# A hybrid conv and dilated-attention encoder: transpositions of the identity ahead of the stretches of products, and an attention core of three borders per head

## The chip, the cores and the metric

The kernel runs on one core of one Trainium2 chip. The metric is the device time of one execution in microseconds (us). The engines are TensorE (PE, with PEld for its weight loads), VectorE (DVE), ScalarE (ACT), GpSimd (POOL) and SyncE (SP), which issues the loads of the weights.

## What is computed

The input is x, 256 tokens of 2048 values, all in float32. Two layers follow, each with a mixer and a gated MLP; then a last norm.

```python
def reference(x, ...):
    for i in range(DEPTH):                      # 2
        h = rmsnorm(x, mix_norm_g[i])
        if i % N_MIXERS == 0:
            x = x + short_conv_mixer(h, ...)    # 2048 -> 6144, conv of width 3, gates, -> 2048
        else:
            x = x + dilated_attention_mixer(h, ...)
        h = rmsnorm(x, ffn_norm_g[i])
        x = x + conv_ffn(h, ...)                # 2048 -> 11264, conv, silu(a) * b, 5632 -> 2048
    return rmsnorm(x, final_norm_g)
```

The attention has 16 heads of 128 values and 3 groups with dilations 1, 4 and 16. Each group has its own q, k and v; scores have an ALiBi bias and a window, and the groups' outputs are mixed by their softmax denominators. The kernel does this as one softmax over 512 columns per query block.

## The kernel before, in words

**Products.** A float32 product is made of three fp32r products: each operand is split into a rounded part and its remainder. `split` (lines 76 to 80) makes the parts: ACT casts (L77), DVE subtracts (L78). `load_w` (82 to 91) loads 1 MB of weights with SP and splits it in two halves of 8 blocks of 128x128, each in one of four `w2` buffers. `mm` (98 to 112) runs over these: per half 8 products high by high (L107), 8 high by low (L109), 8 low by high (L111), each 128x128 by 128x256. So a unit of weights with 16 blocks is 48 products. In the short convolution and in the MLPs the moving operand is `h`, `y` or `a`, always 256 columns of a tile with 512.

**The stages, in order.** `short_conv` (175 to 241): a first block of three outputs while data arrive (`mm1`, L94 to L96), then 45 units over `h` and 16 over `y`. `ffn` (283 to 328) for layer 0: 4 chunks of 22 units over `h` (`up`) and 16 units of 33 products over `a` (`down`), one chunk behind. `attention` (331 to 504). `ffn` for layer 1.

**The norms.** `rms` (161 to 169) sums the squares with one plain float32 matmul (ones by `acc`, 128x256, L163; two records in the profile) and takes the root on DVE and ACT. It stands in the short convolution after its second unit, in each MLP and at the attention's start after the first unit; the products don't wait for it, since its factor is applied to their results.

**Attention.** For each pair of heads there are three `v_unit`s (351 to 385; 96 products each, with weights as the moving operand and `h` as the stationary one, L369 and L374), then twelve `qk_unit`s (387 to 399; 48 products each). The work of a head on scores is queued as tasks, one of which is taken after each unit by `step`: `scores` for group 0 (three fp32r products for each of two query blocks, L404 to L406), `scores` for groups 1 and 2 (two plain float32 matmuls each, 128x128, L418, four records), `softmax` (420 to 431; DVE and ACT only, L423 to L430), `transposes` for each query block (433 to 446; four transpositions of 128x128 float32 to PSUM, L437, copied out by ACT and DVE), and `pv` (448 to 464; six fp32r products, L455, four plain float32 matmuls, L460, eight records, and two copies). A head so interrupts the stream of units six times. `step(3)` after each of the first two units of the output projection and a last loop end the tasks of head 15; then the projection's 16 units over `o`.

**What sets the order.** The kernel is a program of tiles: each engine's order comes from a planner that walks the instructions by their place in the program and takes what it holds to be ready; waits follow from the tiles. `tc.issue_after(ins)` puts an instruction behind another on its engine. The PSUM tile `pt` has one buffer, `s` two, `ps` four, `ot` one.

Of the kernel before, what the change touches and what calls it, by code (L numbers as in the profile page):

```python
# [16 lines left out]
P = 128  # L17
# [21 lines left out]
def encoder_kernel(ctx: ExitStack, tc: tile.TileContext, xT, gs, scw, fcw, dist, w_first, w_in, w_so, w_v, w_qk, w_ao, w_up, w_dn, out):  # L39
# [73 lines left out]

    tp.tile([P, TPAD], F32, name="padt", tag="padt", bufs=1)

    def new_ps():
        return pp.tile([P, 2 * T], F32, name="ps", tag="ps", bufs=4)[:, :T]

# [41 lines left out]

    def rms():
        ps = pp.tile([P, 2 * T], F32, name="stat", tag="s", bufs=2)
        pe.matmul(ps[:, :T], ones, acc, start=True, stop=True)  # L163
        v = tp.tile([P, T], F32, name="v", tag="tmp", bufs=1)
        dve.tensor_scalar(v, ps[:, :T], 1.0 / D, EPS, op0=ALU.mult, op1=ALU.add)
        sd = tp.tile([P, T], F32, name="sd", tag="sq")
        act.activation(sd, v, AF.Sqrt)
        dve.reciprocal(rr, sd)
        newton(rr, v, tp.tile([P, T], F32, name="t", tag="sq"))

    def add_to_x(ps, j):
        dve.tensor_add(x[:, j, :], x[:, j, :], ps)
# [2 lines left out]
    def short_conv():  # L175
        with tc.tile_pool(name="sc", bufs=1) as sp:
            y = sp.tile([P, KT, 2 * T], F32R, name="y")

            def gate(j, es):
                u, c, b = es  # L180
# [24 lines left out]
            for j in range(1, KT):  # L205
                es = []
                for part in range(3):
                    w = load_w(w_in[3 * j + part - 3], KT)
                    if j == 1 and part == 0:
                        first = []  # L210
                        for i in range(3):
                            e = tp.tile([P, T], F32, name="e", tag=f"e{i}")
                            act.copy(e, pss[i])
                            first.append(e)
                        with tc.issue_after(ins.ins):
                            for k in range(KT):
                                squares(k)
                    ps = new_ps()
                    ins = mm(ps, w, h, range(KT))
                    if j == 1 and part == 1:  # L220
                        with tc.issue_after(ins.ins):
                            rms()
                        for e in first:
                            dve.tensor_mul(e, e, rr)
                        gate(0, first)
                        nc.sync.dma_start(fcw_sb, fcw)
                    if j == 1 and part == 0:
                        e = tp.tile([P, T], F32, name="e", tag="e0")
                        act.copy(e, ps)
                        es.append(e)  # L230
                        continue
                    if j == 1 and part == 1:
                        dve.tensor_mul(es[0], es[0], rr)
                    es.append(scaled(ps, f"e{part}", rr))
                gate(j, es)
# [47 lines left out]
    def ffn(l, nxt, halves):  # L283
        with tc.tile_pool(name=f"ff{l}", bufs=1) as sp:

            def up(c):
                a = sp.tile([P, CH, 2 * T], F32R, name="a", tag="a", bufs=2)
                for i in range(CH):
                    f = c * CH + i
                    cs = []  # L290
                    for part in range(2):
                        w = load_w(w_up[l, 2 * f + part], KT)
                        ps = new_ps()
                        mm(ps, w, h, range(KT))
                        if f == 0 and part == 0:
                            rms()
                        e = scaled(ps, f"e{part}", rr)
                        cv = sp.tile([P, T], F32, name="cv", tag=f"cv{part}", bufs=2)
                        conv(cv, e, fcw_sb[:, l, part * NF + f, :])
                        if part == 0:  # L300
                            act.activation(cv, cv, AF.Silu)
                        cs.append(cv)
                    dve.tensor_mul(cs[0], cs[0], cs[1])
                    split(a[:, i, :T], a[:, i, T:], cs[0])
                return a

            def down(c, a):
                for j in range(KT):
                    w = load_w(w_dn[l, c, j], CH)
                    ps = new_ps()  # L310
                    if c == NCH - 1 and nxt == 4:
                        last(ps, w, a, j)
                        continue
                    mm(ps, w, a, range(CH))
                    add_to_x(ps, j)
                    if c == NCH - 1:
                        ready(j, nxt, halves)

            a = up(0)
            for c in range(1, NCH):  # L320
                b = up(c)
                down(c - 1, a)
                a = b
            if nxt == 4:

                warm = tp.tile([P, 2], F32, name="warm", tag="den")
                act.activation(warm, f32(a[:, CH - 1, :2]), AF.Sqrt, bias=eps[:, 0:1], scale=0.0)
            down(NCH - 1, a)


    def attention():
        with tc.tile_pool(name="att", bufs=1) as sp:
            o = sp.tile([P, H, 2 * T], F32R, name="o")
            ds = sp.tile([P, 2, 2 * T], F32, name="ds")
# [13 lines left out]
                    pe.transpose(ps[:, :P], rp[:, i * P : (i + 1) * P], ident)  # L348
                    dve.tensor_copy(rc[:, i : i + 1], ps[:, 0:1])

            def v_unit(hp, g):

                first = hp == 0 and g == 0
                if g == 0:
                    v = sp.tile([P, 2, 2, T], F32R, name="v", tag="v0", bufs=2)
                else:
                    v = sp.tile([P, 2, T], F32, name="v", tag=f"v{g}", bufs=2)
                ps = [new_ps(), new_ps()]
                for k0 in range(0, KT, 8):
                    raw = wp.tile([P, 8, T], F32, name="rawv", tag="raw", bufs=RAW)  # L360
                    nc.sync.dma_start(raw, w_v[3 * hp + g, :, k0 * T : (k0 + 8) * T])
                    for k1 in range(k0, k0 + 8, 4):
# [8 lines left out]
                                    )  # L371
                        for k in range(k1, k1 + 4):
                            for i in range(2):
                                pe.matmul(  # L374
                                    ps[i], h[:, k, T + i * P : T + (i + 1) * P], w2[:, k - k1, 0, :],
                                    start=False, stop=k == KT - 1,
                                )
                if first:
                    norms()
                for i in range(2):  # L380
                    e = tp.tile([P, T], F32, name="e", tag="e0") if g == 0 else v[:, i, :]
                    act.mul(e, ps[i], rc[:, i : i + 1])
                    if g == 0:
                        split(v[:, i, 0, :], v[:, i, 1, :], e)
                vs[hp, g] = v

            def qk_unit(hd, g, part):
                w = load_w(w_qk[(hd * G + g) * 2 + part], KT)
                ps = new_ps()
                mm(ps, w, h, range(KT))  # L390
                r = rp if part else rq
                if g == 0:
                    e = scaled(ps, "e1", r)
# [2 lines left out]
                else:  # L396
                    t = sp.tile([P, T], F32, name="qkf", tag=f"qkf{part}", bufs=3)
                    scaled(ps, "e1", r, t)
                heads[hd, g, part] = t

            def mm3(out, l, lc, r, rc_, start, stop):
                lh, ll = l[:, lc], l[:, lc.start + T : lc.stop + T]
                rh, rl = r[:, rc_], r[:, rc_.start + T : rc_.stop + T]
                pe.matmul(out, lh, rh, start=start, stop=False)  # L404
                pe.matmul(out, lh, rl, start=False, stop=False)  # L405
                pe.matmul(out, ll, rh, start=False, stop=stop)  # L406

            def scores(hd, g):
                q, k = heads.pop((hd, g, 0)), heads.pop((hd, g, 1))
# [2 lines left out]
                for i in range(2):  # L412
                    s = heads[hd][i]
                    c = slice(i * P, (i + 1) * P)
                    if g == 0:
                        mm3(s[:, :T], q, c, k, slice(0, T), True, True)
                    else:
                        pe.matmul(s[:, T + (g - 1) * P : T + g * P], q[:, c], k[:, c], start=True, stop=True)  # L418

            def softmax(hd, i):  # L420
                s = heads[hd][i]
# [26 lines left out]
            def pv(hd):  # L448
# [7 lines left out]
                for g in (1, 2):  # L456
                    v = vs[hd // 2, g]
                    for i in range(2):
                        q = slice(i * P, (i + 1) * P)
                        pe.matmul(ot[:, q], v[:, i, c], tf[:, g - 1, q], start=False, stop=g == 2 and i == 1)  # L460
                hi, lo = (o[:, hd, z : z + T].rearrange("p (m i) -> p i m", i=2) for z in (0, T))
                src = ot.rearrange("p (i m) -> p i m", i=2)
                act.copy(hi, src)
                dve.tensor_sub(lo, src, f32(hi))

            def step(n=1):
                for _ in range(n):
                    if tasks:
                        tasks.popleft()()

            for hp in range(H // 2):
                for g in range(G):
                    v_unit(hp, g)
                    step()
                for hd in (2 * hp, 2 * hp + 1):
                    for g in range(G):
                        qk_unit(hd, g, 0)
                        step()
                        qk_unit(hd, g, 1)
                        step()  # L480
                        tasks.append(lambda hd=hd, g=g: scores(hd, g))
                    tasks.append(lambda hd=hd: (softmax(hd, 0), softmax(hd, 1)))
                    tasks.append(lambda hd=hd: transposes(hd, 0))
                    tasks.append(lambda hd=hd: transposes(hd, 1))
                    tasks.append(lambda hd=hd: pv(hd))
            first = []
            for j in range(2):
                w = load_w(w_ao[j], KT)
                ps = new_ps()
                mm(ps, w, o, range(KT - 1))  # L490
                step(3)
                first.append((ps, w))
            while tasks:
                step()
            for j in range(KT):
                if j < 2:
                    ps, w = first[j]
                    mm(ps, w, o, range(KT - 1, KT))
                else:
# [4 lines left out]
                ready(j, 3, False)  # L504

    short_conv()
    ffn(0, 2, True)
    attention()
    ffn(1, 4, False)


# [80 lines left out]
```

## Time and profile before

| | |
|---|---|
| median of 3 runs | 2787.13 us (2785.28 to 2811.06) |
| profiled execution, device time | 2787.24 us |
| its span, first to last instruction | 2784.0 us |
| mean granted TensorE clock | 0.998 |
| PE, DVE, ACT busy share of the span | 99%, 65%, 49% |
| HBM | 186 GB/s over the span |

A row of the timeline gives start, length, engine, line, operation and operands, and the count of instructions merged in it; the length runs to the end of the last one, and matmuls overlap, so the pace is read from starts. In a row of the chain the length is the time from one step to the next, so the lengths add up. In a row of the windows, the number behind x counts every instruction that lies in the stretch, those cut by its edges too.

### The profile page before, as it was taken

What the parts mean: (1) busy time and instruction counts of PE and PEld (TensorE: products, weight loads), DVE (VectorE), ACT (ScalarE), POOL (GpSimd) and SP (SyncE); (2) the same over time, 40 slices, a digit from 0 to 9 for tenths busy, and PEclk for the clock granted to TensorE, in tenths of its full rate; (3) what the DMA queues carried; (4) which work ended last, traced back from release to release, by engine and by line L of the source; (5) the groups of instructions that cost most, each with busy time, mean ns of one, the idle gap of its engine ahead of it and who ended that gap; (6) DMA issues with size and microseconds to landing.
All of it is one profiled execution on the core that took longest, in us unless ns stands there. A gap on an engine that the chain in (4) does not pass through costs nothing.

```text
span 2784.0 us, 55141 instructions
## 1 busy us (share of the span) xinstructions
PE 2766.3 (99%) x24020; PEld 2763.4 (99%) x24020; DVE 1802.8 (65%) x2553; ACT 1354.9 (49%) x1860; POOL 0.7 (0%) x6
## 2 busy tenths in 40 slices
PE   9999999999999999999999999999999999999998
PEld 8999999999999999999999999999999999999998
DVE  7666677775767757555555555555677775766755
ACT  6444455554545546444444444444455554544545
POOL 0000000000000000000000000000000000000000
PEclk9999999999999999999999999999999999999999
DMA  7555555556556556555554555555455556556554
GB/s 263 183 190 188 182 194 190 195 173 220 193 171 214 173 192 219 184 178 168 179 184 167 179 172 180 169 180 176 172 183 197 196 171 212 196 171 221 178 182 143
DMA packets 79874, 520.41 MB, mean 187 GB/s; under 512 B 9104, under 2 KB 10256, under 8 KB 28816
## 3 DMA queue, kind: packets, MB, share of 16 engines
q1 hardware_dynamic: 79488, 516.37, 54.0%
q8 instruction: 187, 3.06, 0.4%
q10 hardware_dynamic: 144, 0.52, 0.0%
q14 instruction: 55, 0.45, 0.0%
HBM read 514.76 MB, written 2.10 MB: 186 GB/s over the span
## 4 chain that ended last, share of the span: by engine, by line
PE 98%; DVE 1%; DMA 0%; issue 0%; ACT 0%; SPq 0%; DVEq 0%; ACTq 0%
PE ps L107 29%; PE ps L111 29%; PE ps L109 29%; PE ps L369 6%; PE ps L374 3%; PE ot L460 1%; PE s L418 1%; PE pt L437 1%; PE ot L455 0%; DMA raw<-in_w_first 0%; DVE x L278 0%; DVE acc L147 0%; PE s L405 0%; PE s L406 0%; PE s L404 0%
## 5 line engine op out<-in xcount | busy, mean ns | idle before, releaser
L78 DVE TENSOR_TENSOR w<-raw,w 128x1024 fp32r<-128x1024 f32 (+1 forms) x954 | 1082.3, 1135 | 689.2 <-ACT w L77 677.7
L77 ACT CAST w<-raw 128x1024 fp32r<-128x1024 f32 (+1 forms) x954 | 930.1, 980 | 1116.0 <-PE ps L111 895.7
L107 PE MATMUL ps<-h,w 128*128 128x256 f32 x5072 | 692.7, 279 | 0.0
L111 PE MATMUL ps<-h,w 128*128 128x256 f32 x5072 | 686.3, 278 | 0.0
L109 PE MATMUL ps<-h,w 128*128 128x256 f32 x5072 | 686.1, 278 | 0.0
L107 PEld LDWEIGHTS ps<-h,w 128*128 128x128 f32 x5072 | 630.1, 188 | 0.2
L109 PEld LDWEIGHTS ps<-h,w 128*128 128x128 f32 x5072 | 629.5, 188 | 0.0
L111 PEld LDWEIGHTS ps<-h,w 128*128 128x128 f32 x5072 | 629.3, 188 | 0.0
L111 PE MATMUL ps<-a,w 128*128 128x256 f32 x1408 | 201.3, 276 | 0.0
L107 PE MATMUL ps<-a,w 128*128 128x256 f32 x1408 | 201.2, 276 | 0.0
L109 PE MATMUL ps<-a,w 128*128 128x256 f32 x1408 | 201.2, 276 | 0.0
L369 PE MATMUL ps<-w2v,h 128*128 128x256 f32 x1536 | 194.1, 279 | 0.0
L78 DVE TENSOR_TENSOR w2v<-rawv,w2v 128x1024 fp32r<-128x1024 f32 x96 | 117.5, 1224 | 115.8 <-ACT w2v L77 115.8
L369 PEld LDWEIGHTS ps<-w2v,h 128*128 128x128 f32 x1536 | 184.0, 188 | 0.1
L111 PEld LDWEIGHTS ps<-a,w 128*128 128x128 f32 x1408 | 178.6, 188 | 0.0
L107 PEld LDWEIGHTS ps<-a,w 128*128 128x128 f32 x1408 | 178.6, 188 | 0.0
L109 PEld LDWEIGHTS ps<-a,w 128*128 128x128 f32 x1408 | 178.6, 188 | 0.0
L77 ACT CAST w2v<-rawv 128x1024 fp32r<-128x1024 f32 x96 | 100.7, 1049 | 123.2 <-PE ps L374 78.8
L122 DVE TENSOR_TENSOR e<-ps,rr 128x256 f32<-128x256 f32 x220 | 93.4, 425 | 57.0 <-PE ps L111 51.1
L127 ACT ACTIVATE cv<-e,fcw_sb 128x256 f32<-128x256 f32 x176 | 104.9, 597 | 1.0 <-DVE e L122 1.0
L374 PE MATMUL ps<-w2v,h 128*128 128x256 f32 x768 | 103.9, 278 | 0.0
L374 PEld LDWEIGHTS ps<-w2v,h 128*128 128x128 f32 x768 | 95.3, 188 | 0.0
(123 smaller groups left out, 1523.1 us busy)
## 6 DMA issues: line engine op xcount, KB each, us to landing
raw<-in_w_up SPq DMA_DIRECT2D x176, 1024.0 KB, 4.8
raw<-in_w_qk SPq DMA_DIRECT2D x96, 1024.0 KB, 4.8
raw<-in_w_dn SPq DMA_DIRECT2D x128, 704.0 KB, 4.1
rawv<-in_w_v SPq DMA_DIRECT2D x48, 1024.0 KB, 5.1
raw<-in_w_in SPq DMA_DIRECT2D x45, 1024.0 KB, 4.8
raw<-in_w_so SPq DMA_DIRECT2D x16, 1024.0 KB, 4.8
raw<-in_w_ao SPq DMA_DIRECT2D x16, 1024.0 KB, 4.9
raw<-in_w_first SPq DMA_DIRECT2D x3, 384.0 KB, 5.1
```

The costliest lines, as they stand in the source:

```text
L77: ins = act.copy(hi, src)
L78: dve.tensor_sub(lo, src, f32(hi))
L107: pe.matmul(ps, w2[:, 0, parts[k][1], :], a[:, k, :T], start=k == 0, stop=False)
L109: pe.matmul(ps, w2[:, 0, parts[k][1], :], a[:, k, T:], start=False, stop=False)
L111: ins = pe.matmul(ps, w2[:, 1, parts[k][1], :], a[:, k, :T], start=False, stop=k == n - 1)
L122: dve.tensor_mul(e, ps, r)
L127: act.activation(c, e, AF.Identity, bias=w[:, 3:4], scale=w[:, 1:2])
L369: pe.matmul(ps[i], h[:, k, i * P : (i + 1) * P], w2[:, k - k1, z, :], start=k == z == 0, stop=False)
L374: pe.matmul(ps[i], h[:, k, T + i * P : T + (i + 1) * P], w2[:, k - k1, 0, :], start=False, stop=k == KT - 1,)
L418: pe.matmul(s[:, T + (g - 1) * P : T + g * P], q[:, c], k[:, c], start=True, stop=True)
L437: pe.transpose(pt[:, n, :], b[:, n * P : (n + 1) * P], ident)
L460: pe.matmul(ot[:, q], v[:, i, c], tf[:, g - 1, q], start=False, stop=g == 2 and i == 1)
```

## The change

A new helper, `settle`, issues one transposition of the identity (128x128, float32, to `pt`, read by nobody) behind a given instruction on PE. It is called after each `rms` matmul but that of the attention, in the MLP behind the first unit of chunks 1 to 3, ahead of the first `v_unit` of each pair of heads, behind the third `v_unit` where no task is queued (the first pair), behind each head's scores, and behind two `pv`s at the end. That makes 1 call in the short convolution, 8 in the MLPs and 27 in the attention.

The tasks of a head become three: the `pv` of the head before with all of this head's scores, one `settle` and the softmax; then the two `transposes`, a unit apart each. At the end three units of the projection are begun instead of two, with head 15's scores, transpositions and `pv` between them. The short convolution's pool gets a tile of 64 bytes per partition behind `y`.

```diff
+    def settle(ins):
+        ps = pp.tile([P, 4, P], F32, name="pt", tag="pt", bufs=1)
+        with tc.issue_after(ins.ins):
+            return pe.transpose(ps[:, 0, :], ident, ident)
...
             y = sp.tile([P, KT, 2 * T], F32R, name="y")
+            sp.tile([P, 16], F32, name="pad")
...
                         with tc.issue_after(ins.ins):
-                            rms()
+                            settle(rms())
...
-                        mm(ps, w, h, range(KT))
+                        ins = mm(ps, w, h, range(KT))
+                        if i == 0 and part == 0 and c:
+                            settle(ins)
                         if f == 0 and part == 0:
-                            rms()
+                            settle(rms())
...
+                if ins is not None:
+                    settle(ins)
                 ps = [new_ps(), new_ps()]
...
+            def core(hd):
+                for g in range(G):
+                    ins = scores(hd, g)
+                settle(ins)
+                softmax(hd, 0)
+                softmax(hd, 1)
+
+            def core_after(hd):
+                pv(hd - 1)
+                core(hd)
...
                 for g in range(G):
-                    v_unit(hp, g)
+                    ins = v_unit(hp, g, ins if g == 0 else None)
+                    if g == 2 and not tasks:
+                        settle(ins)
                     step()
...
-                        tasks.append(lambda hd=hd, g=g: scores(hd, g))
-                    tasks.append(lambda hd=hd: (softmax(hd, 0), softmax(hd, 1)))
+                    if hd == H - 1:
+                        continue
+                    tasks.append(lambda hd=hd: core_after(hd) if hd else core(hd))
                     tasks.append(lambda hd=hd: transposes(hd, 0))
                     tasks.append(lambda hd=hd: transposes(hd, 1))
-                    tasks.append(lambda hd=hd: pv(hd))
+            settle(pv(H - 2))
             first = []
-            for j in range(2):
+            for j in range(3):
                 w = load_w(w_ao[j], KT)
                 ps = new_ps()
-                mm(ps, w, o, range(KT - 1))
-                step(3)
+                mm(ps, w, o, range(8))
+                if j == 2:
+                    settle(pv(H - 1))
+                mm(ps, w, o, range(8, KT - 1))
+                if j == 0:
+                    core(H - 1)
+                if j == 1:
+                    transposes(H - 1, 0)
+                    transposes(H - 1, 1)
                 first.append((ps, w))
```

## Rows read from the trace of the kernel before

**Rows 1.** The page: PE's busy time, and the chain that ended last.

```profile
PE 2766.3 (99%) x24020; PEld 2763.4 (99%) x24020; DVE 1802.8 (65%) x2553; ACT 1354.9 (49%) x1860; POOL 0.7 (0%) x6
...
PE 98%; DVE 1%; DMA 0%; issue 0%; ACT 0%; SPq 0%; DVEq 0%; ACTq 0%
```

**Rows 2.** PE in six stretches: length, PE busy (instructions), clock, DMA share, GB/s.

```profile
50.00:370.00 320.00, 320.00 (x2719) 1.00 0.53 186
400.00:1080.00 680.00, 680.00 (x6003) 1.00 0.56 192
1091.42:2057.38 965.96, 965.72 (x8314) 1.00 0.52 177
1198.26:1306.65 108.39, 108.39 (x939) 1.00 0.51 175
1976.00:2050.00 74.00, 74.00 (x631) 1.00 0.54 188
2070.00:2760.00 690.00, 690.00 (x6090) 1.00 0.56 190
```

**Rows 3.** Timeline of PE: the norm's matmul in the short convolution and in layer 0's MLP.

```profile
44.34 0.70 PE L163 MATMUL stat<-acc,ones 128*128 128x256 f32 x2
...
378.43 0.60 PE L163 MATMUL stat<-acc,ones 128*128 128x256 f32 x2
```

**Rows 4.** Timeline of PE: the six borders of a head (scores, transpositions, pv).

```profile
1256.99 0.28 PE L404 MATMUL s<-qk 128*128 128x256 f32 x1
...
1257.70 1.11 PE L107 MATMUL ps<-h,w 128*128 128x256 f32 x8
...
1263.36 0.61 PE L418 MATMUL s<-qkf 128*128 128x128 f32 x4
1263.72 1.19 PE L107 MATMUL ps<-h,w 128*128 128x256 f32 x8
1264.75 1.11 PE L109 MATMUL ps<-h,w 128*128 128x256 f32 x8
...
1286.87 0.60 PE L437 MATMUL pt<-ident,b 128*128 128x128 f32 x4
1287.22 1.17 PE L107 MATMUL ps<-h,w 128*128 128x256 f32 x8
1288.23 1.07 PE L109 MATMUL ps<-h,w 128*128 128x256 f32 x8
1289.13 1.07 PE L111 MATMUL ps<-h,w 128*128 128x256 f32 x8
...
1298.66 0.88 PE L455 MATMUL ot<-pT,v 128*128 128x256 f32 x6
...
1300.19 1.19 PE L107 MATMUL ps<-h,w 128*128 128x256 f32 x8
```

**Rows 5.** Chain of waits in the attention's start: v products before and after transpositions.

```profile
1100.17 1.88 PE ps L369 x16
...
1110.73 0.41 PE stat L348 x2
...
1112.53 1.81 PE ps L369 x16
```

**Rows 6.** Chain of waits: from the third v unit to the qk units.

```profile
1231.51 0.91 PE ps L374 x8
1232.42 0.94 PE ps L107 x8
```

**Rows 7.** Instructions on tile pt: duration ns min/median/max.

```profile
L437 PE MATMUL pt<-ident,b x128: 270/272/329, 1178.5 to 1970.8; 128*128 128x128 f32 x128
```

**Rows 8.** The page's weight splits, and timeline of DVE: a head's softmax.

```profile
L78 DVE TENSOR_TENSOR w<-raw,w 128x1024 fp32r<-128x1024 f32 (+1 forms) x954 | 1082.3, 1135 | 689.2 <-ACT w L77 677.7
...
1275.66 1.27 DVE L423 SCALAR_TENSOR_TENSOR b<-ds,s 128x512 f32<-128x512 f32 x2
...
1279.70 0.88 DVE L430 TENSOR_SCALAR b<-b,inv 128x512 f32<-128x512 f32 x2
```

More of the change, by code (lines that the diff above doesn't have):

```diff
@@ L162, in rms @@
         ps = pp.tile([P, 2 * T], F32, name="stat", tag="s", bufs=2)
-        pe.matmul(ps[:, :T], ones, acc, start=True, stop=True)
+        ins = pe.matmul(ps[:, :T], ones, acc, start=True, stop=True)
         v = tp.tile([P, T], F32, name="v", tag="tmp", bufs=1)
@@ L169, in rms @@
         newton(rr, v, tp.tile([P, T], F32, name="t", tag="sq"))
+        return ins
     def add_to_x(ps, j):
@@ L313, in down @@
                         continue
-                    mm(ps, w, a, range(CH))
+                    ins = mm(ps, w, a, range(CH))
                     add_to_x(ps, j)
@@ L317, in down @@
                         ready(j, nxt, halves)
+                return None if nxt == 4 else ins
             a = up(0)
@@ L327, in ffn, with attention @@
                 act.activation(warm, f32(a[:, CH - 1, :2]), AF.Sqrt, bias=eps[:, 0:1], scale=0.0)
-            down(NCH - 1, a)
-    def attention():
+            return down(NCH - 1, a)
+    def attention(ins):
         with tc.tile_pool(name="att", bufs=1) as sp:
@@ L349, in norms, with v_unit @@
                     dve.tensor_copy(rc[:, i : i + 1], ps[:, 0:1])
-            def v_unit(hp, g):
+            def v_unit(hp, g, ins):
                 first = hp == 0 and g == 0
@@ L373, in v_unit @@
                             for i in range(2):
-                                pe.matmul(
+                                m = pe.matmul(
                                     ps[i], h[:, k, T + i * P : T + (i + 1) * P], w2[:, k - k1, 0, :],
@@ L377, in v_unit @@
                                 )
+                                if k == KT - 1:
+                                    ins = m
                 if first:
@@ L385, in v_unit @@
                 vs[hp, g] = v
+                return ins
             def qk_unit(hd, g, part):
@@ L389, in qk_unit @@
                 ps = new_ps()
-                mm(ps, w, h, range(KT))
+                ins = mm(ps, w, h, range(KT))
                 r = rp if part else rq
@@ L399, in qk_unit @@
                 heads[hd, g, part] = t
+                return ins
             def mm3(out, l, lc, r, rc_, start, stop):
@@ L405, in mm3 @@
                 pe.matmul(out, lh, rl, start=False, stop=False)
-                pe.matmul(out, ll, rh, start=False, stop=stop)
+                return pe.matmul(out, ll, rh, start=False, stop=stop)
             def scores(hd, g):
@@ L415, in scores @@
                     if g == 0:
-                        mm3(s[:, :T], q, c, k, slice(0, T), True, True)
+                        ins = mm3(s[:, :T], q, c, k, slice(0, T), True, True)
                     else:
-                        pe.matmul(s[:, T + (g - 1) * P : T + g * P], q[:, c], k[:, c], start=True, stop=True)
+                        ins = pe.matmul(s[:, T + (g - 1) * P : T + g * P], q[:, c], k[:, c], start=True, stop=True)
+                return ins
             def softmax(hd, i):
@@ L459, in pv @@
                         q = slice(i * P, (i + 1) * P)
-                        pe.matmul(ot[:, q], v[:, i, c], tf[:, g - 1, q], start=False, stop=g == 2 and i == 1)
+                        ins = pe.matmul(ot[:, q], v[:, i, c], tf[:, g - 1, q], start=False, stop=g == 2 and i == 1)
                 hi, lo = (o[:, hd, z : z + T].rearrange("p (m i) -> p i m", i=2) for z in (0, T))
@@ L464, in pv, with step @@
                 dve.tensor_sub(lo, src, f32(hi))
[L466 to L469, printed above, removed]
+                return ins
+            def core(hd):
[7 more added lines that the diff above has]
+                core(hd)
+            def step():
+                if tasks:
+                    tasks.popleft()()
             for hp in range(H // 2):
                 for g in range(G):
-                    v_unit(hp, g)
+                    ins = v_unit(hp, g, ins if g == 0 else None)
+                    if g == 2 and not tasks:
+                        settle(ins)
                     step()
@@ L478, in attention @@
                         step()
-                        qk_unit(hd, g, 1)
+                        ins = qk_unit(hd, g, 1)
                         step()
-                        tasks.append(lambda hd=hd, g=g: scores(hd, g))
-                    tasks.append(lambda hd=hd: (softmax(hd, 0), softmax(hd, 1)))
+                    if hd == H - 1:
+                        continue
+                    tasks.append(lambda hd=hd: core_after(hd) if hd else core(hd))
                     tasks.append(lambda hd=hd: transposes(hd, 0))
                     tasks.append(lambda hd=hd: transposes(hd, 1))
-                    tasks.append(lambda hd=hd: pv(hd))
+            settle(pv(H - 2))
             first = []
-            for j in range(2):
+            for j in range(3):
                 w = load_w(w_ao[j], KT)
                 ps = new_ps()
-                mm(ps, w, o, range(KT - 1))
-                step(3)
+                mm(ps, w, o, range(8))
[7 more added lines that the diff above has]
+                    transposes(H - 1, 1)
                 first.append((ps, w))
-            while tasks:
-                step()
             for j in range(KT):
-                if j < 2:
+                if j < 3:
                     ps, w = first[j]
@@ L506, in encoder_kernel @@
     short_conv()
-    ffn(0, 2, True)
-    attention()
+    attention(ffn(0, 2, True))
     ffn(1, 4, False)
```

## The prediction, made before the change was run

> **What bounds the kernel now.** I read the page first. PE is busy for 99% of the span and the chain that ended last lies on PE for 98% of it [rows 1]: nothing else sets the end, and a change counts by what it does to PE's own time. The chain names the product lines, so the next question is what one product costs. I took that from windows laid inside uniform stretches, as length over count (less the two instructions that the edges cut). The short convolution gives 320.00 us over 2717, or 117.8 ns a product; the first MLP 680.00 over 6001, 113.3 ns; the second MLP 690.00 over 6088, 113.3 ns; the output projection 74.00 over 629, 117.6 ns [rows 2]. [...] That is what the reader is to see: a PE at 99% that runs 4% slower in some stretches than in others.
>
> What picks the pace? The timeline shows the switches. After a plain float32 matmul, pace varies: the norm's at 44.34 leaves the slow pace, the norm's at 378.43 the fast one [rows 3, 2]. After a head's plain scores and after its pv the qk products run slow, 0.94 us for 8. After four transpositions they run fast: 1288.23 to 1289.13 is 0.90 us for 8, 113 ns each [rows 4]. Each of the 32 bursts of transpositions but the last, which has only four products behind it, is followed so, and so are the two single transpositions in the attention's start: 16 v products take 1.88 us before and 1.81 us after [rows 5]. The pace also changes without any such border where the operands change roles: fast v products are followed by slow qk products, 0.91 and then 0.94 us for 8 [rows 6]. Within a role it holds: each MLP keeps it through its 152 units, from h to a and back.
>
> **The change part by part.**
>
> *Short convolution.* One transposition behind the norm's matmul. The 45 units less the two begun before it, and 16 of y, make 2832 products behind it, all slow now. At the fast pace each gains 4.45 ns: 2832 x 4.45 = 12.6 us. That y keeps the pace I take from the MLPs, where a does, a tile of the same row length at the head of a stage's pool.
>
> *MLPs.* They are fast already, so 8 transpositions there gain nothing and cost their slots.
>
> *Attention, products.* One cycle of two heads lasts 108.39 us [rows 2] and has 3 x 96 + 12 x 48 = 864 products, 97.9 us at the fast pace. The borders of a head, beyond the products beside them [rows 4]: group 0's scores 1257.70 - 1256.99 = 0.71 us; each plain score 0.36, and 0.09 more in the first 8 products behind it (1.03 for 0.94), 0.45, twice; each burst of transpositions 0.35 and 0.10 (1.01 for 0.91), 0.46, twice; pv 1.53 and again 0.09, 1.62. The sum is 4.15, for two heads 8.30 us. What is left, 108.39 - 97.9 - 8.3 = 2.2 us, is slow products, some 490 of 864. Eight cycles make 17.5 us; the first v unit, slow up to the two transpositions, 0.4 us more; the projection's 768 products and the next MLP's first unit of 48, 816 x 4.45 ns = 3.6 us. Together 21.5 us. From above it agrees: 965.96 us [rows 2] less 7728 products at 113.3 ns (875.6), less 16 x 4.15 (66.4), leaves 24.0, of which the two norms and the short waits at the tail take the 2.5. In the changed order every stretch of v, qk and o products begins behind a transposition, so all of it should go but the 60 v products between the norm (which gets none) and its two transpositions: 0.3 us stays. Gain 21.2 us.
>
> *Attention, borders.* Fewer borders save nearly nothing. The entry costs that merge away are not there: a plain score of four records costs 0.45 us, four records of 0.11, and pv's 14 instructions cost 1.62, 14 slots of 0.115. So a merged core costs what its parts cost. I put the merging at nothing.
>
> *A transposition.* Four cost 0.46 us with their entry, 0.115 to 0.12 each [rows 4]. A lone one is in no row. Below, 0.09 (0.36 us for four records between starts); above, its whole duration without overlap, 0.27 [rows 7]. I take 0.118, nearest to the burst, where the first of four shows no larger gap than the rest. 36 of them make 4.2 us (bounds 3.2 and 9.7). A gain below nothing is excluded, since each is an extra instruction on the engine that sets the end.
>
> [...]
>
> *Softmax nearer to its transpositions.* Now two units lie between a head's last scores and its transpositions (bias at 1275.66, transpositions at 1286.87 [rows 8, 4]). In the new order one unit lies between them, for 8 heads a qk unit of 48 x 113.3 ns = 5.4 us, for the others a v unit of 10.9. The chain from the bias at 1275.66 to the first scaled weights at 1279.70 + 0.44 is 4.5 us [rows 8], beside weight splits on the same DVE. If DVE has just begun a split (1.14 us) when the scores end, 5.6 us against 5.4 plus the transposition: no wait, or some tenths. PE takes its queue in order, so what waits behind the transpositions is the next unit's products. I take 0, and up to 0.5 us for 8 heads, 4 us, into the range. The pv and the next scores need tiles written units before: no wait.
>
> *Tail and start.* Head 15's steps keep a unit or half a unit of products between them; the few tenths of waiting there go or stay. But three begun units hold three of the four weight buffers, so the fourth unit's second half is split late: up to 0.5 us. I count 0. The 64 bytes behind y move only the weight tiles of the first block, which is mostly fed by loads; if its products took a faster pace it would be worth under 1 us. 0.
>
> *The sum.* 12.6 + 21.2 - 4.2 = 29.6 us off the profiled execution's 2787.24 us (its span of 2784.0 with 3.2 us around it): 2757.6 us. The median of the runs, 2787.13, is the same to 0.1 us. I predict 2757.5 us, 1.06% faster. A measurement of this kernel can tell about 1%, 27.9 us, from no change, which puts the line at 2759.3: the forecast lies just beyond it.
>
> **The rivals.**
>
> *The fast pace doesn't hold everywhere.* A role change flips the pace [rows 6], and y and o come behind h with no transposition at the change (y), or behind a new kind of border (o). For: y and o have never been seen fast over a stretch; both are slow now. Against: a in the MLPs changes nothing. If both stay slow, 768 x 4.45 ns twice, 6.8 us, is lost: 2764. One alone: 2761.
>
> *The softmax becomes late.* For: half the distance. Against: 4.5 us in 5.4, and the planner fills. With 1 us for 15 heads: 2772; with 0.5 for 8: 2762.
>
> *The pace belongs to the operands' places, not to what came before.* Then transpositions cost and give nothing: 2787.2 + 4.2 = 2791. Against it speak the same qk products, slow before a burst and fast behind it [rows 4]. [...]
>
> *A lone transposition resets PE to the slow pace* (the other side). All rows have two or four together, and none stands directly behind a plain float32 matmul. The MLPs run fast with none; at their first transposition they would fall to the slow pace: 2 x 6280 x 4.45 ns = 55.9 us lost, with 4.2 for the slots: 2847 us at least. It decides as soon as over 6700 of the MLPs' 12,600 products are slowed, where the other gains are eaten up (29.6 us over 4.45 ns). Against: what follows is set at the change from transposition to product, and that change is the same behind one as behind four.
>
> *More than forecast.* The core's 12 fp32r products a head at 113 for 119 ns (1.2 us), the first block (1 us), cheaper slots (1 us): 2754.
>
> **How the numbers follow.** Forecast within 4 us 0.60 (three quarters of it beyond the line); more than forecast 0.10; pace only in part 0.12; late softmax 0.10; no effect 0.03; slow reset 0.05. So faster by over 1%: 0.57; within 1%: 0.38; slower by over 1%: 0.05. The range goes down to 2751, where the cheapest slots and the small gains meet, and up to 2771, which takes in a lost y and o with some waits. The slow reset and the case of no effect stay outside.
>
> **What would show it.** Right: windows inside the short convolution and the projection give 113.3 ns a product, a cycle of two heads lasts 106.5 us (864 x 113.3 ns + 8.3 + three transpositions), the MLPs are unchanged but for 0.5 us each. Each lone transposition takes 0.11 to 0.13 us from start to start. Wrong: 117.8 ns behind any transposition, above all over y; idle PE time ahead of L437's successor that DVE's scaled weights end; MLP windows above 114 ns.

## The result and the profile after

The changed kernel took 2806.5 us (median of 20 runs, 2799.1 to 2811.4) against 2793.6 for the kernel before beside it (20 runs, 2784.6 to 2811.1): a ratio of 1.004, interval 1.0023 to 1.0057. A little slower, where 1.06% faster was forecast; 2806.5 lies outside the range.

The times of both kernels fall into groups, and that is part of the finding. In that comparison the kernel before ran at 2785 to 2787 or at 2800 to 2802 us, once at 2811; in two others, further down, at 2810 to 2813 or at 2824 to 2827. A median of such a mixture moves with the shares of its groups, so the ratio is not the change's alone. Of the three runs shown ahead of the prediction two, and the profile, were of the lowest group.

PE in stretches of the changed kernel, laid as in [rows 2], columns as there:

```profile
50.00:370.00 320.00, 320.00 (x2720) 1.00 0.54 187
400.00:495.00 95.00, 95.00 (x840) 1.00 0.57 196
505.00:680.00 175.00, 175.00 (x1488) 1.00 0.53 185
690.00:866.00 176.00, 176.00 (x1497) 1.00 0.54 185
880.00:1095.00 215.00, 215.00 (x1899) 1.00 0.54 186
1107.55:2066.16 958.61, 958.12 (x8337) 1.00 0.52 179
1318.47:1426.04 107.57, 107.57 (x941) 1.00 0.52 177
```

Length over count less two again. The short convolution still runs at 117.7 ns a product, though a transposition now stands at its head. In layer 0's MLP the stretch behind the norm runs at 113.4 ns, the two behind the first two chunk transpositions at 117.8, the last at 113.3. Before, the whole MLP ran at 113.3. Layer 1's MLP has the same pattern. The attention lasts 958.6 us for 965.6 of the same extent, a cycle of two heads 107.57 for 108.39.

The timeline shows the entry to the first slow stretch, then a head's core and the burst a unit behind it:

```profile
499.21 1.07 PE L111 MATMUL ps<-h,w 128*128 128x256 f32 x8
500.12 0.27 PE L120 MATMUL pt<-ident 128*128 128x128 f32 x1
500.15 1.19 PE L107 MATMUL ps<-h,w 128*128 128x256 f32 x8
501.17 1.11 PE L109 MATMUL ps<-h,w 128*128 128x256 f32 x8
...
1290.03 0.27 PE L120 MATMUL pt<-ident 128*128 128x128 f32 x1
1290.05 1.19 PE L107 MATMUL ps<-h,w 128*128 128x256 f32 x8
1291.08 1.10 PE L109 MATMUL ps<-h,w 128*128 128x256 f32 x8
...
1295.80 0.60 PE L455 MATMUL pt<-ident,b 128*128 128x128 f32 x4
1296.15 1.17 PE L107 MATMUL ps<-h,w 128*128 128x256 f32 x8
1297.15 1.07 PE L109 MATMUL ps<-h,w 128*128 128x256 f32 x8
```

Eight products span 1.10 to 1.11 us at the slow pace and 1.07 at the fast one. At 500.12 the products ahead run at 113.3 ns, those behind at 117.8: the lone transposition took the pace away. At 1290.03 the one at the core's end leaves slow products; the softmax's own four, a unit later, bring the fast pace.

Not everywhere, though. Between two v units the same four leave the slow pace that they find, 7 times of 7 in this profile (ahead of the first such burst 8 products take 0.94 us, 1235.58 to 1236.52, and behind it 0.94 us, 1238.85 to 1239.79):

```profile
1235.58 1.10 PE L387 MATMUL ps<-w2v,h 128*128 128x256 f32 x8
1236.52 0.60 PE L455 MATMUL pt<-ident,b 128*128 128x128 f32 x4
1236.88 2.13 PE L382 MATMUL ps<-w2v,h 128*128 128x256 f32 x16
1238.85 1.10 PE L387 MATMUL ps<-w2v,h 128*128 128x256 f32 x8
1239.79 2.05 PE L382 MATMUL ps<-w2v,h 128*128 128x256 f32 x16
```

By stage, from the norms' starts in both profiles: ahead of the first norm 44.3 before and 45.7 us after; short convolution 334.1 and 334.2; MLPs 713.1 and 727.7, twice; attention 965.6 and 958.6. The sum of the differences, 1.3 + 0.1 + 2 x 14.6 - 7.0 = 23.6 us, is, to 0.1, the difference of the spans, 2807.5 - 2784.0 = 23.5. The first term is the run's and not the change's: in a second profile of the changed kernel (the run "once more", below) the first norm starts at 44.3 us too. So the question was why products behind a transposition run slow, and what the times' groups are.

### The profile page after: what moved, and what is told of

It reads as the page before. It is cut to its first block, busy times and chain, and to the rows that moved or that the text cites. A ratio compares the mean times of both kernels' runs of the same rounds, so it can differ in the third digit from the quotient of the medians.

```text
span 2807.5 us, 55211 instructions
## 1 busy us (share of the span) xinstructions
PE 2788.3 (99%) x24056; PEld 2785.3 (99%) x24056; DVE 1810.5 (64%) x2553; ACT 1353.0 (48%) x1860; POOL 0.7 (0%) x6
## 4 chain that ended last, share of the span: by engine, by line
PE 98%; DVE 1%; DMA 0%; issue 0%; ACT 0%; SPq 0%; DVEq 0%; ACTq 0%
PE ps L107 29%; PE ps L109 29%; PE ps L111 29%; PE ps L382 6%; PE ps L387 3%; PE s L435 1%; PE ot L478 1%; PE pt L455 1%; DMA raw<-in_w_first 0%; PE ot L473 0%; DVE x L286 0%; PE pt L120 0%; DVE acc L153 0%; PE s L422 0%; PE s L421 0%
## 5 line engine op out<-in xcount | busy, mean ns | idle before, releaser
L109 PE MATMUL ps<-a,w 128*128 128x256 f32 x1408 | 204.4, 278 | 0.0
L107 PE MATMUL ps<-a,w 128*128 128x256 f32 x1408 | 204.3, 278 | 0.0
L111 PE MATMUL ps<-a,w 128*128 128x256 f32 x1408 | 204.3, 279 | 0.0
L111 PEld LDWEIGHTS ps<-a,w 128*128 128x128 f32 x1408 | 181.5, 188 | 0.0
L109 PEld LDWEIGHTS ps<-a,w 128*128 128x128 f32 x1408 | 181.4, 188 | 0.0
L107 PEld LDWEIGHTS ps<-a,w 128*128 128x128 f32 x1408 | 181.3, 188 | 0.0
```

Of the source, the lines that this page charges most:

```text
L107: pe.matmul(ps, w2[:, 0, parts[k][1], :], a[:, k, :T], start=k == 0, stop=False)
L109: pe.matmul(ps, w2[:, 0, parts[k][1], :], a[:, k, T:], start=False, stop=False)
L111: ins = pe.matmul(ps, w2[:, 1, parts[k][1], :], a[:, k, :T], start=False, stop=k == n - 1)
```

## The experiments

Theory A: every border in the stream of products draws the pace anew; the products behind it start at 117.8 ns and slip to 113.3 within some ten products, or stay slow up to the next border. Rivals: the slow stretches come from the run (B), the number of transpositions decides (C), the attention's gain is the transpositions' (D).

**Without the chunk transpositions.**

```diff
-                        if i == 0 and part == 0 and c:
-                            settle(ins)
```

> The changed kernel without the transpositions in the MLP chunks (6 of 36); the one behind each norm stays. Theory A (each border decides the pace anew: the products behind it start at 117.8 ns and slip to 113.3 within some ten products or stay slow up to the next border): both MLPs run at 113.3 ns throughout, as behind the norm in both profiles, and the time falls by the four slow stretches, 4 x 1570 x 4.45 ns = 28 us, to about 2779 us. Rival B (the slow stretches of the MLPs come from the run, not from the transpositions): slow stretches stay, the time stays at 2800 to 2810 us.

Measured: 2786.0 us, where 2779 was expected; ten runs in two groups, 2776.6 to 2778.8 and 2793.1 to 2795.9; ratio 0.998, 0.995 to 1.001. The profile, of the upper group, has PE in the short convolution and the two MLPs:

```profile
50.00:360.00 310.00, 310.00 (x2738) 1.00 0.55 194
370.00:1080.00 710.00, 710.00 (x6031) 1.00 0.54 185
2070.00:2760.00 690.00, 690.00 (x6090) 1.00 0.55 192
```

No pace changes inside a stage any more; but now the short convolution is fast (113.3 ns), layer 0's MLP slow throughout (117.8), layer 1's fast. All three have the same border at the head, the norm's matmul with one transposition. So B falls for the chunk stretches, and A holds in a form I hadn't expected: the draw behind a norm comes out differently in the same place.

**The chunk transpositions alone, in the kernel before.**

```diff
...
-                        mm(ps, w, h, range(KT))
+                        ins = mm(ps, w, h, range(KT))
+                        if i == 0 and part == 0 and c:
+                            settle(ins)
```

> The kernel before with the six transpositions in the MLP chunks alone. Theory A: the MLPs have slow stretches behind some of them, two per MLP if the timing at the border is that of the changed kernel: +28 us against a run of the kernel before with fast MLPs, about 2814 us. Rival B: as the kernel before, within 1 us for the six slots.

Measured: 2820.9 us (2817.3 to 2826.9); ratio 1.010, 1.006 to 1.014. Of the six chunk stretches of the profile five are slow and one is fast (layer 0's second, in the row below at 113.3 ns); the two behind the MLPs' norms, with no transposition, are slow as well, and the short convolution is fast.

```profile
690.00:850.00 160.00, 160.00 (x1414) 1.00 0.56 190
```

**Four transpositions for each one, in the changed kernel.**

```diff
-        with tc.issue_after(ins.ins):
-            return pe.transpose(ps[:, 0, :], ident, ident)
+        for n in range(4):
+            with tc.issue_after(ins.ins):
+                ins = pe.transpose(ps[:, n, :], ident, ident)
+        return ins
```

> The changed kernel with four transpositions wherever it has one. Rival C (four in a row leave the fast pace and one does not, since in both profiles each burst of four among h products is followed by the fast pace): short convolution, MLPs and projection at 113.3 ns, 28 + 12.6 + 3.4 us less, and behind the cores too, against 108 slots more of 0.115 us (12.4 us): about 2770 us. Theory A: a draw again, some stretches slow, others fast, with no rule by the number: between 2780 and 2825 us.

Measured: 2782.8 us in two groups (2781.2 to 2783.1, 2790.7 to 2793.3); ratio 0.997, 0.995 to 0.9997. Fast behind 5 of 6 chunk bursts, all 8 cores among h products, all 7 among v products, and in the projection; slow behind the first pair's third v unit; behind the norms' matmul with four, one of three is fast. So C is right in most places, but four in a row are no guarantee: the sixth chunk burst stands between h products as the other five do.

```profile
2176.36 0.60 PE L121 MATMUL pt<-ident 128*128 128x128 f32 x4
2176.71 1.19 PE L107 MATMUL ps<-h,w 128*128 128x256 f32 x8
2177.74 1.11 PE L109 MATMUL ps<-h,w 128*128 128x256 f32 x8
```

The attention is 957.7 us, 0.9 less than the changed kernel's: 81 more slots of 0.115 us, 9.3, eat nearly all that the pace gives.

**One to four, shuffled, behind 86 units of each MLP in the kernel before.**

```diff
...
+                        if f:
+                            settle(ins, COUNTS[2 * f + part])
```

> The kernel before with one, two, three or four transpositions behind each unit of the MLPs' up products, in a shuffled order that is the same in both layers: 87 borders per layer, all from h products to h products. Rival C: all borders of four fast, borders of one slow. Theory A: each number has both outcomes; where the outcome hangs on the program alone, the two layers agree border by border, and where it hangs on the run they don't. Slots: 2 x 217 x 0.115 = 50 us.

Measured: 2837.1 us, one run. Of the 86 borders a layer (the expectation says 87) three lead to `a` products and are fast. Counting the pace behind the 83 that stand between h products, from the starts in the trace:

| transpositions | layer 0: fast of all | layer 1: fast of all |
|---|---|---|
| 1 | 2 of 21 | 2 of 21 |
| 2 | 12 of 22 | 11 of 22 |
| 3 | 20 of 20 | 20 of 20 |
| 4 | 20 of 20 | 20 of 20 |

The layers agree in 76 of 83; the seven others are all borders of two. Three borders of the timeline, with four, three and two:

```profile
523.11 0.60 PE L122 MATMUL pt<-ident 128*128 128x128 f32 x4
523.46 1.17 PE L108 MATMUL ps<-h,w 128*128 128x256 f32 x8
524.47 1.07 PE L110 MATMUL ps<-h,w 128*128 128x256 f32 x8
...
529.00 0.49 PE L122 MATMUL pt<-ident 128*128 128x128 f32 x3
529.25 1.17 PE L108 MATMUL ps<-h,w 128*128 128x256 f32 x8
530.26 1.07 PE L110 MATMUL ps<-h,w 128*128 128x256 f32 x8
...
534.80 0.38 PE L122 MATMUL pt<-ident 128*128 128x128 f32 x2
534.93 1.19 PE L108 MATMUL ps<-h,w 128*128 128x256 f32 x8
535.96 1.10 PE L110 MATMUL ps<-h,w 128*128 128x256 f32 x8
```

**Short products in their place.** The same counts, with fp32r products of 128 columns that nobody reads.

```diff
-                ins = pe.transpose(ps[:, n, :], ident, ident)
+                ins = pe.matmul(ps[:, n, :], w[0][0][:, 0, n, :], h[:, n, :P], start=True, stop=True)
```

> As the run with one to four transpositions behind each MLP up unit, in the same order, but with fp32r products of 128 columns (of the unit's own weights) in place of the transpositions. If it is the transposition that leads to the fast pace, each border here leaves the pace that was there or a slow one, with no rule by count. If it is the run of short instructions, three and four lead to the fast pace, in 40 of 40 each as with transpositions, and one doesn't.

Measured: 2840.7 us, one run; behind one, 4 of 21 fast in each layer; behind two, 22 of 22; three, 20 of 20; four, 20 of 20. Nothing here is a transposition, so a run of short instructions is enough; but the kind counts too, since two transpositions led to the fast pace in 23 of 44 cases and two short products in all 44. By the starts each takes its 0.11 us as a transposition does:

```profile
528.44 0.33 PE L122 MATMUL pt<-h,w 128*128 128x128 f32 x2
528.61 1.14 PE L108 MATMUL ps<-h,w 128*128 128x256 f32 x8
529.59 1.07 PE L110 MATMUL ps<-h,w 128*128 128x256 f32 x8
...
534.12 0.56 PE L122 MATMUL pt<-h,w 128*128 128x128 f32 x4
534.51 1.13 PE L108 MATMUL ps<-h,w 128*128 128x256 f32 x8
```

Behind a lone one the pace turned over every time: all 34 borders with 113.3 ns ahead had 117.8 behind, and all 8 with 117.8 ahead had 113.3 behind.

**The core of three borders with no added transposition.**

```diff
     def settle(ins):
-        ps = pp.tile([P, 4, P], F32, name="pt", tag="pt", bufs=1)
-        with tc.issue_after(ins.ins):
-            return pe.transpose(ps[:, 0, :], ident, ident)
+        return ins
```

> The changed kernel with no added transposition at all: the attention core of three borders, the tail and the 64 bytes stay. Theory A: a core now ends in plain float32 matmuls, behind which every h unit was slow in the kernel before; its attention is the changed kernel's less 27 slots (3.1 us), plus or minus what the draws at the v units give: 950 to 960 us against 965.6 before and 958.6 after. The MLPs and the short convolution are all fast or all slow, each as a whole, by the draw behind the norm. Rival D (the fall of 7 us in the attention came from the transpositions): 965 us or more.

Measured: 2789.5 us, one run, with the short convolution and one MLP fast and the other MLP slow. The attention and a cycle in it:

```profile
1106.57:2060.76 954.19, 953.93 (x8310) 1.00 0.52 179
1531.49:1638.33 106.84, 106.84 (x939) 1.00 0.52 178
```

954.2 us, 11.4 less than before and 4.4 less than with the transpositions. Another profile of this core with no transposition at cores and v units (the run with few bursts, below) has 950.9 us with a fast projection, which is worth about 3. D falls: the attention's gain is the merging's, and the 27 transpositions take some of it back.

**The kernel before once more.**

> The kernel before, unchanged, for one more profile. Theory A says what its two modes are, at 2785 and 2801 us: the draws behind the norms. At 2785 the short convolution is slow and both MLPs fast, as in the profile shown. At 2801 the short convolution is fast (12.6 us less) and one MLP slow throughout (28 us more): +15.4 us. The profile shows one of the two; a third pattern at one of these times would speak against it.

Measured: 2809.8 us, one run, which is neither 2785 nor 2801. PE in the short convolution and the two MLPs:

```profile
50.00:370.00 320.00, 320.00 (x2719) 1.00 0.53 185
400.00:1080.00 680.00, 680.00 (x6002) 1.00 0.56 192
2070.00:2760.00 690.00, 690.00 (x5860) 1.00 0.54 185
```

The same program, but layer 1's MLP is now slow throughout (690.00 over 5858, 117.8 ns): 27.9 us more, and the projection fast, 3.1 us less; with 0.9 us less at the two ends it comes to 2807.9 - 2784.0 = 23.9 of span. So groups of times are draws behind norms; this shows that for 2810 us. The others fit by sums alone: 2801 is 2785.5 - 12.6 + 27.9, and 2825 is 2785.5 - 12.6 + 2 x 27.9 - 3.1. I didn't see those two in a profile of this kernel; the run above without added transpositions has the draws of 2801, and its 2789.5 is 2801 less the attention's 11.4. Nor is it the chip alone: the kernel before ran at 2785 to 2802 us, once at 2825, beside the first four experiments, and at 2811 to 2827 beside these, on a chip of the same number.

**Three for each one, and behind the norms a unit later.** None stands in the chunks any more, and one alone ahead of the v units from the second pair on. In the MLP:

```diff
...
-                        if i == 0 and part == 0 and c:
+                        if f == 0 and part == 1:
                             settle(ins)
                         if f == 0 and part == 0:
-                            settle(rms())
+                            rms()
```

> The changed kernel with three transpositions in place of one, behind cores, pv and the last v unit; none in the MLP chunks; behind a norm not at the norm but one unit later, between h products; one only ahead of the v units. Theory A with the rule of the counts (three or four between h products lead to the fast pace, one doesn't): short convolution 321.6 us, MLPs 713.5 each in every run, so no second mode 15 us away; attention 958.6 less 11.2 for the units behind cores and the projection, plus 36 slots (4.1 us): 951.5; with 43.5 ahead and 14 behind 2757 us of span, 2759 us. Rival (what stands behind a border doesn't hold from run to run): the two modes stay.

Measured: 2779.0 us, four runs at 2779 to 2780 and two at 2767 and 2769; ratio 0.984, 0.981 to 0.987, beside runs of the kernel before at 2810 to 2827. I missed by 20 us. Both MLPs are fast in the profile, but in the short convolution the planner had put the burst straight behind the norm's matmul, and that stage is slow (117.8 ns): 12.8 us. The two quicker runs lie some 11 us lower, about what a fast short convolution is worth; no profile shows them. And in the attention (957.9 us) the v units behind cores with three transpositions are slow, where behind four, or none, they were fast; and those behind the lone ones ahead are slow, which were fast in the changed kernel. Among v products my rule of the counts doesn't hold.

**No transposition but four bursts of three.** One in the short convolution, one in each MLP, one behind the last `pv` (the expectation counts five).

```diff
...
+                    if j == 2 and part == 0:
+                        settle(ins)
```

> The core of three borders without transpositions at cores, v units and chunks, and five bursts of three in the whole program, each apart from the norm's matmul: behind the first unit of the short convolution's third block, behind the second unit of each MLP, and behind the last two heads' end (one burst behind the last pv). Theory A with the rule of the counts: short convolution 321.6 us and two units at most slow, MLPs 713.7 each, attention 954.2 less 3 for a fast projection, 951.5: a span of 2759 us, 2761 us, and one mode only, whatever the draws behind the norms are. Rival (bursts of three can fail at the short convolution): 2773 us in some runs.

Measured: 2774.1 us, three runs at 2760 to 2761 and three at 2787 to 2788; ratio 0.984, 0.980 to 0.989, beside runs of the kernel before at 2810 to 2826. The profile is of the upper group: short convolution fast, layer 1's MLP fast, layer 0's slow behind its burst of three (117.8 ns). A burst can fail, here in three of six runs by the times.

```profile
380.00:1095.00 715.00, 715.00 (x6073) 1.00 0.54 185
```

**The changed kernel once more.**

> The changed kernel, unchanged, beside the kernel before on this chip. Theory A: lone transpositions in the MLPs leave most of the six chunk stretches slow on any chip, 2800 to 2811 us, while the kernel before takes whatever its draws behind the three norms give: 2785, 2801, 2811 or 2825 us. So the ratio of the two hangs on the draws of the kernel before, and can lie on either side of 1.

Measured: 2801.5 us (2798.7 to 2811.1) beside 2811.3 for the kernel before (2809.9 to 2826.4): ratio 0.996, 0.994 to 0.998. The same pair with the other sign, since the kernel before, by its times, drew a slow MLP in every run there. In the changed kernel's profile four of six chunk stretches are slow again, but not the same four.

**Short bursts behind three units in a row.** As the run with few bursts, with four short products for the three transpositions in the short convolution and the MLPs.

```diff
...
+                        if (f, part) in ((0, 1), (1, 0), (1, 1)):
+                            short(ins, w)
```

> As the run with few bursts, but in the short convolution and the MLPs four fp32r products of 128 columns in place of three transpositions, behind three units in a row each (short convolution: third block; MLPs: units 2 to 4), so that one failed draw is mended by the next. Theory A with the rule of the counts (62 of 62 fast behind bursts of two to four short products, in each of two layers): all three stages at 113.3 ns in every run, the time 2760 to 2762 us in one mode. Rival (a stage's pace is decided at its head and a burst soon behind it can fail in any run): runs at 2773 or 2788 us as in the run with few bursts.

Measured: 2763.4 us, six runs from 2762.9 to 2764.7, one group; ratio 0.990, 0.987 to 0.993, beside runs of the kernel before at 2785 to 2811. PE in the three stages:

```profile
70.00:360.00 290.00, 290.00 (x2561) 1.00 0.56 194
390.00:1070.00 680.00, 680.00 (x6003) 1.00 0.56 193
2055.00:2735.00 680.00, 680.00 (x6002) 1.00 0.56 191
```

113.3 ns in all three, though all three draws behind the norms were slow in that profile, and one burst of the nine failed and was mended by the next:

```profile
50.34 0.56 PE L129 MATMUL pt<-h,w 128*128 128x128 f32 x4
...
51.73 1.11 PE L109 MATMUL ps<-h,w 128*128 128x256 f32 x8
...
56.44 0.56 PE L129 MATMUL pt<-h,w 128*128 128x128 f32 x4
...
57.80 1.07 PE L109 MATMUL ps<-h,w 128*128 128x256 f32 x8
```

All six runs lie below every run of both kernels. It is one comparison of six runs, so it doesn't show that three bursts never all fail.

## Why the prediction was wrong

The bound and the two paces were read rightly (the granted clock is 1.00 in every stretch shown of both kernels), and so was the price of a slow product: 4.45 ns, by which 117.8 and 113.3 differ before rounding, times the slow products of a stage, with the slots, gives the differences of the stages above to about a microsecond. What sets the pace was read wrongly.

The step that failed stands in the rival I gave 0.05: "what follows is set at the change from transposition to product, and that change is the same behind one as behind four." It isn't. Among h products, in the run that shuffled the counts, 38 of 42 lone transpositions led to the slow pace and 80 of 80 bursts of three and four to the fast one. The burst isn't certain either: two of those in the MLPs failed in other runs. Every row I had showed bursts of four, or two. I had noted that a lone one is in no row, bounded its price, and not its effect.

A second step failed behind it: the MLPs' fast pace was taken for a property of the program. It was a draw of one execution: in the second profile of the kernel before layer 1's MLP is slow throughout. So even the sign of the measured difference hangs on how often the kernel before drew a slow MLP beside it (1.004 in one comparison, 0.996 in another). Of the three runs shown one stood 24 us above the other two, and I passed over it, though no step of mine could have made it.

By the terms of the sum:
- *Short convolution, -12.6.* 0.1 more. A slow draw behind norm and transposition; behind norms the number didn't help either. (The count of 2832 came out right, though the norm stands behind the third unit: 42 units of h, 16 of y, and the MLP's first unit.)
- *MLPs, +0.5 each.* 14.6 more each: two stretches of 1584 slow products, 14.1, and the slots. The reset to the slow pace that the rival named, for half of the products instead of all.
- *Attention, -21.2 and 3.2 for slots.* 7.0 less. The products behind each core stayed slow, and so did the v products behind the softmax's bursts and most of the projection: by the starts about 2750 products of 7728, where 60 were expected and about 4790 were slow before. The merging, counted at nothing, is worth 11.4 alone: not by entry costs, where the estimate was right, but because fewer plain float32 borders left fewer slow stretches in these profiles. With the core alone about 2390 are slow, 2400 fewer than before, 10.7 us at 4.45 ns.
- *A slot, 0.118.* Right: at 500.12 the starts are 118, 27 and 201 ns apart up to the second product, which less two products at 117.8 makes 0.11 us.
- *Softmax a unit nearer.* Right: the burst starts at 1295.80 with no wait in the timeline. That PE keeps its order shows at 1110.73 of the kernel before: a transposition waited 0.23 us for DVE there, and four v products, the last of a run of 16 whose weights were split by 1108.68, started behind it.
- *The first block.* Its products behind the first loads ran at 113.3 ns (117.8 before), but PE then waited 0.75 us for the squares ahead of the norm, so nothing came of it.

The point at which a lone reset decides was put at 6700 slowed products; 6336 chunk products were slow, and with the gains that hadn't come, that was enough.

## What to carry to other kernels

Where a PE-bound kernel has two paces for one instruction, count the pace by stretches in several executions before trusting either: one profile shows a draw. A remedy must be seen in the form in which it is to be used, count and neighbours included, and a stage whose pace is decided at one border wants a second and a third chance to change it, cheap ones: here four 128-column products, 0.4 us together, behind three units in a row. One by itself, in this kernel, mostly led to the slow pace or turned the pace over.

## What the runs showed of the hardware

In these profiles full-width products run at 113.3 or 117.8 ns at one granted clock of 1.00, hold either pace for thousands of products (in the profile before 2832 in a row at 117.8 ns in the short convolution, 6288 at 113.3 in layer 1's MLP), and change it at a border or where the operands change roles (v to qk, 0.91 and then 0.94 us for 8 in [rows 6]). Behind a border they start slow: the gap from the second product to the third is 116 to 122 ns in all 166 stretches of 40 or more products that follow a border later than 40 us in the profiles of the kernel before and of the changed kernel. In 34 of the 83 of these that turn fast within 25 products one gap of 121 to 123 ns comes first (at 873.49 of the changed kernel: 117, 118, 122, 118, 114, then 113 ns).

Between h products, in the two runs with shuffled counts, two or more short products of 128 columns brought the fast pace in 124 of 124 cases, three or four transpositions in 80 of 80, two transpositions in 23 of 44. A lone transposition led to the slow pace in 38 of 42 cases, whatever stood ahead; a lone short product turned the pace over in 42 of 42. In other runs bursts failed too: one of the six chunk bursts of four, one of the two MLP bursts in the run with few bursts, and one of the nine short bursts in the last run. Between v products the rule doesn't hold: the softmax's four left the slow pace 7 times of 7 in the changed kernel. Behind the norm's matmul the draw varies from run to run: in the kernel before, layer 1's MLP ran at 113.3 ns in one profile and at 117.8 in the other. Why the number decides, what the pace consists of, why a burst fails, and why the rule differs among v products stays open: no run here looks inside PE.
